# Five instead of four of the eight pairs of k tiles by seven products in the feed-forward units

## The chip, the cores and the metric

The kernel runs on one core of a Trainium2 chip. The metric is the device time of one execution in microseconds (us), lower is better. Before the change it is 2174.18 us, the median of three runs (2173.97 to 2175.04). The core has TensorE for matmuls (PE in the profile, its weight loads PEld), VectorE (DVE), ScalarE (ACT), GpSimd (POOL) and SyncE (SP), which issues the transfers from device memory. Each engine has its own queue, worked off in order.

## What is computed

Two layers of an encoder on 256 tokens of 2048 channels, all in float32. Each layer is a mixer (attention and a gated recurrence in the first, pooling and grouped attention in the second) and then a feed-forward, each with a residual sum and a normalisation. The change lies in the feed-forwards:

```python
def swiglu(x, w_gate, w_up, w_down):
    return (jax.nn.silu(x @ w_gate) * (x @ w_up)) @ w_down
...
x = layer_norm(DN_ALPHA * x + y, ln_mix_g[layer], ln_mix_b[layer])
f = swiglu(x, ffn_w_gate[layer], ffn_w_up[layer], ffn_w_down[layer])
x = layer_norm(DN_ALPHA * x + f, ln_ffn_g[layer], ln_ffn_b[layer])
```

`w_gate` and `w_up` are 2048 x 5632, `w_down` is 5632 x 2048.

## The kernel before

**Products.** A float32 operand is split into a high part, rounded to the type that TensorE takes (F32R), and a low part, the rest. `mm3` (line 289) makes one product of a 128 x 128 block of x, as the stationary operand, and a 128 x 512 block of weights from three matmuls: low by high, high by high, high by low. Weights come as "halves": two blocks of 128 x 512, 512 KB. `load_half` (line 147) transfers one into one of four buffers `raw`, ScalarE copies the high part into `whi` (line 122), VectorE subtracts it for the low part `wlo` (line 123). During the units the ring of `whi` and `wlo` has four buffers.

**The feed-forward's chunks.** The 5632 hidden columns are 11 chunks of 512. Chunks 0 and 1 are done by `whole`, plainly. Chunks 2 to 10 are "units" (`unit`, line 455), in rounds of two, `((2, 3), (0, 1)), ((4, 5), (2, 3))` and so on: while the units of a round make gate and up of two chunks, the down projection of the two chunks before runs in between, as steps of a generator (`down_steps`, line 508; a step is one half, 12 matmuls). There are nine units per layer, 18 in all.

**A unit.** It has four accumulator banks: c11 and c21 for the gate of the first and the second 128 tokens, c12 and c22 for the up. The 16 k tiles of x are eight pairs. A pair that is done plainly takes 2 token blocks x 2 k tiles x 2 (gate, up) = 8 products, 24 matmuls, from two halves. A pair done "by seven products" (pairs 4 to 7, `SEVEN`) uses sums: of x, the forms e, f, g, h, and of the weights. It comes in two parts.

- *The first phase.* `load_seven` (line 433) transfers the pair's four blocks in one piece of 1 MB (`rs`, two buffers), and VectorE makes sums of them in `z` (one buffer; lines 444 to 446). The gate block and three sums are split into `sh` and `sl` (two buffers each), the fourth sum, the "edge", into `zh` and `zl` (four buffers), which must live until the second phase. Four products (`BEGIN`, line 453) go into the four banks. After each pair come as many down steps as `GAPS` says: 2, 1, 1, 2. After the last pair ScalarE and VectorE combine the banks (lines 474 to 479): c12 is rewritten by line 476, c21 by line 478, c22 by line 479.
- *The second phase.* For each of the four seven-product pairs, one half of it is loaded again and split, and three products follow, into c11, c12 and (with the edge) c21. In between stand the four plain pairs. Then line 503 and 504 make silu(gate) times up; its transposition into `y` is left to a list, `flips`, which the next unit works off after its first two down steps.

So a unit has 48 + 132 matmuls of its own, and 96 of eight down steps: two before the flips, six in the gaps.

**Forms.** `forms_of` (line 409) makes e to h from x for the four pairs during the second chunk of `whole`, two steps at a time each time that a half has been used. Its tiles `xs` and `fs` take the room of `rs` and `z`.

**Buffers of y.** The transposed results y of the chunks, and before that the four groups of the mixer's result, share four buffers of 4 KB a partition for the high and the low part each (`new_yT`).

**Order of work.** The program is written in the order above, with raised priority for loads and splits (`tc.high_priority`). A planner then orders every engine's queue at build time: it plays the program through with costs of its own and takes at each point the first instruction that is ready, so matmuls of down steps and of later products fill in where weights are not ready. On the chip each queue keeps that order.

Of the kernel before, what the change touches and what calls it, by code (L numbers as in the profile page):

```python
# [12 lines left out]
F32R = mybir.dt.float32r  # L13
# [5 lines left out]
P = 128  # L19
T = 256  # L20
# [3 lines left out]
NCH = 512  # L24
# [45 lines left out]

ROUNDS = (((2, 3), (0, 1)), ((4, 5), (2, 3)), ((6, 7), (4, 5)), ((8, 9), (6, 7)), ((10,), (8,)))
LAST = (9, 10)
SEVEN = (4, 5, 6, 7)
PLAIN = (0, 1, 2, 3)
GAPS = (2, 1, 1, 2)


@with_exitstack
def trunk(ctx: ExitStack, tc: tile.TileContext, a, out):
# [5 lines left out]
    ap_ = ctx.enter_context(tc.tile_pool(name="acts", bufs=1))  # L85
# [11 lines left out]
    def bank(tag, bufs):  # L97
        return banks["pool"].tile([P, NCH], F32, tag=tag, name=tag, bufs=bufs)
# [22 lines left out]
    def split(hi, lo, src):  # L121
        nc.scalar.copy(hi, src)  # L122
        return nc.vector.tensor_tensor(lo, src, hi.bitcast(F32), op=sub).ins  # L123
# [55 lines left out]
    def half_done(n=1):  # L179
        for entry in list(later):  # L180
            entry[0] -= n
            if entry[0] <= 0:
                later.remove(entry)
                entry[1]()
# [70 lines left out]
        return xh, xl  # L255

    def new_yT():
        yh = ap_.tile([P, 4, T], F32R, tag="yTh", name="yTh", bufs=4)
        yl = ap_.tile([P, 4, T], F32R, tag="yTl", name="yTl", bufs=4)
        return yh, yl  # L260

    def x_lhs(xT):
        return lambda tok, k: (xT[0][tok][:, k, :], xT[1][tok][:, k, :])
# [18 lines left out]
    def split_tile(pool, shape, src, tag, bufs=1):  # L282
        hi = pool.tile(shape, F32R, tag=tag + "h", name=tag + "h", bufs=bufs)
        lo = pool.tile(shape, F32R, tag=tag + "l", name=tag + "l", bufs=bufs)
        if src is not None:
            split(hi, lo, src)
        return hi, lo
# [8 lines left out]
    def at(pair, *ix):  # L296
        return pair[0][ix], pair[1][ix]
# [108 lines left out]
        return xT  # L406


    def forms_of(sp, xT, out):

        n = len(SEVEN)
        xs = sp.tile([P, NT, 2 * n, P], F32, tag="rs", name="xs", bufs=2)
        fs = sp.tile([P, 4, n, P], F32, tag="z", name="fs", bufs=1)
        yield
        for t in range(NT):
            s = slice(2 * SEVEN[0], 2 * SEVEN[0] + 2 * n)
            nc.vector.tensor_tensor(xs[:, t], xT[0][t][:, s, :].bitcast(F32), xT[1][t][:, s, :].bitcast(F32), op=add)
            yield
        x11, x12, x21, x22 = (xs[:, t, e : 2 * n : 2, :] for t in range(2) for e in range(2))
        e, f, g, h = (fs[:, i] for i in range(4))  # L420
        nc.vector.tensor_tensor(e, x22, x21, op=sub)
        nc.vector.tensor_tensor(f, e, x11, op=add)
        yield
        nc.vector.tensor_tensor(g, x11, x21, op=sub)
        nc.vector.tensor_tensor(h, x12, f, op=sub)
        yield
        hi, lo = split_tile(sp, [P, 4, n, P], fs, "fm")
        for i, p in enumerate(SEVEN):
            x = lambda t, k: (xT[0][t][:, k, :], xT[1][t][:, k, :])
            e, f, g, h = (at((hi, lo), slice(None), j, i) for j in range(4))  # L430
            out[p] = {"11": x(0, 2 * p), "12": x(0, 2 * p + 1), "22": x(1, 2 * p + 1), "e": e, "f": f, "g": g, "h": h}

    def load_seven(sp, src):

        with tc.high_priority(offset=400):
            raw = sp.tile([P, 4, NCH], F32, tag="rs", name="rs", bufs=2)
            hi = sp.tile([P, 4, NCH], F32R, tag="sh", name="sh", bufs=2)
            lo = sp.tile([P, 4, NCH], F32R, tag="sl", name="sl", bufs=2)
            zh = sp.tile([P, NCH], F32R, tag="zh", name="zh", bufs=4)
            zl = sp.tile([P, NCH], F32R, tag="zl", name="zl", bufs=4)  # L440
            z = sp.tile([P, 4, NCH], F32, tag="z", name="z", bufs=1)
            last_load[0] = nc.sync.dma_start(raw, src).ins
            nc.scalar.copy(hi[:, 0], raw[:, 0])
            nc.vector.tensor_tensor(z[:, :2], raw[:, 0:3:2], raw[:, 3:4].to_broadcast([P, 2, NCH]), op=add)
            nc.vector.tensor_tensor(z[:, 2], z[:, 0], raw[:, 2], op=add)  # L445
            nc.vector.tensor_tensor(z[:, 3], z[:, 2], raw[:, 1], op=add)
            nc.vector.tensor_tensor(lo[:, 0], raw[:, 0], hi[:, 0].bitcast(F32), op=sub)
            split(hi[:, 1:], lo[:, 1:], z[:, :3])
            split(zh, zl, z[:, 3])
        return lambda i: (hi[:, i, :], lo[:, i, :]), (zh, zl)  # L450
# [4 lines left out]
    def unit(sp, w, lhs, forms, y, down, flips):  # L455


        def run(n):
            for _ in range(n):
                next(down, None)  # L460

        run(2)
        while flips:
            flips.pop(0)()
        b = {n: bank("un", 4) for n in ("c11", "c12", "c22", "c21")}
        edge = {}
        for i, (p, gap) in enumerate(zip(SEVEN, GAPS)):
            wt, edge[p] = load_seven(sp, w[p])
            for j, x, name in BEGIN:
                mm3(b[name], forms[p][x], wt(j), i == 0, i == len(SEVEN) - 1)  # L470
            if i == len(SEVEN) - 1:
                with tc.high_priority(offset=1000):
                    g0, g1 = (sp.tile([P, NCH], F32, tag=n, name=n, bufs=1) for n in ("g0", "g1"))
                    nc.scalar.copy(g0, b["c11"])
                    nc.vector.tensor_tensor(g1, b["c12"], g0, op=sub)
                    nc.vector.tensor_tensor(b["c12"], g1, b["c22"], op=sub)
                    nc.vector.tensor_tensor(g1, g1, b["c21"], op=sub)
                    nc.scalar.activation(b["c21"], g1, AF.Copy, scale=-1.0)
                    nc.vector.tensor_tensor(b["c22"], g1, b["c22"], op=sub)
            run(gap)  # L480

        left = {n: 4 * len(PLAIN) // 2 + (n != "c22") * len(SEVEN) for n in b}

        def product(name, x, wt):
            left[name] -= 1
            mm3(b[name], x, wt, False, left[name] == 0, skip_group_check=True)

        for p, s in zip(PLAIN, SEVEN):
            hi, lo = load_half(w[s][:, 1:3])
            for i, x, name in ((0, "12", "c11"), (1, "h", "c12")):  # L490
                product(name, forms[s][x], (hi[:, i, :], lo[:, i, :]))
            product("c21", forms[s]["22"], edge[s])
            half_done()
            for n, ks in ((0, (2 * p, 2 * p + 1)), (1, (2 * p + 1, 2 * p))):
                hi, lo = load_half(w[p][:, 2 * n : 2 * n + 2])
                for tok in range(NT):
                    for kk in range(2):
                        product(f"c{tok + 1}{n + 1}", lhs(tok, ks[kk]), (hi[:, kk, :], lo[:, kk, :]))
                half_done()
        with tc.high_priority(offset=1000):  # L500
            for tok in range(NT):
                g = sp.tile([P, NCH], F32, tag=f"g{tok}", name=f"g{tok}", bufs=1)
                nc.scalar.activation(g, b[f"c{tok + 1}1"], AF.Silu)
                nc.vector.tensor_tensor(g, g, b[f"c{tok + 1}2"], op=mult)
                s = slice(tok * P, (tok + 1) * P)
                flips.append(lambda g=g, s=s: transpose4(g, y[0][:, :, s], y[1][:, :, s], 1000))
# [31 lines left out]
    def ffn(layer, xT, res, mix_pool, close_mix, keep, last):  # L538
        lhs = x_lhs(xT)
        w = a[f"gu{layer}"]  # L540
# [33 lines left out]
        forms, making, sps, flips = {}, [], [], []  # L574

        def make():
            with tc.issue_after(low[-1]):
                for _ in range(2):
                    if next(making[0], "end") == "end":
                        return  # L580
            later.append([1, make])

        def change_rooms():
            close_mix()
            sps.append(later_pool(stack, f"sp{layer}"))
            making.append(forms_of(sps[0], xT, forms))
            later.append([1, make])

        groups = {c: None for c in range(2)}
# [20 lines left out]
        yl = y_lhs([groups[c] for c in LAST])  # L610
# [459 lines left out]


    xT = new_xT()
    yT = [new_yT() for _ in range(4)]
    with tc.tile_pool(name="wab", bufs=1) as wab:
        rings.append((wab, 2))
        with tc.tile_pool(name="ab", bufs=1) as mp:
# [7 lines left out]
    def later_pool(stack, name):  # L1084
        return stack.enter_context(tc.tile_pool(name=name, bufs=1, reuse_waits="tile"))
# [20 lines left out]

    consts = []
    xT = layer_end(0, a["ab_out"], AB_OUT_GROUPS, yT, False)
    yT = [new_yT() for _ in range(4)]
    with tc.tile_pool(name="cd", bufs=1, reuse_waits="tile") as mp:  # L1110
        cd_mixer(mp, consts, xT, yT)
    layer_end(1, a["cd_out"], CD_OUT_GROUPS, yT, True)
# [115 lines left out]
```

## Time and profile before

| | |
|---|---|
| median of three runs | 2174.18 us |
| the profiled execution: its own time | 2174.19 us |
| its span, first to last instruction | 2172.4 us |
| granted TensorE clock, mean | 0.997 |
| TensorE busy | 2152.8 us, 99% |
| VectorE busy | 1634.4 us, 75% |
| ScalarE busy | 1188.5 us, 55% |
| moved by DMA | 458.40 MB, 211 GB/s over the span |

The profile is one execution. Its time is 1.8 us over its span; work is counted against the time, positions are in us from the span's start. In a row of a group, "x72" is the number of instructions, then stand the busy time in all, the mean of one in ns, and the idle time of the engine before them with what ended it. In a row of the timeline stand the start, the duration, the engine, the line and what is written from what; a bracket gives the idle time before it and its releaser. A matmul's own duration (389 ns) overlaps with its neighbours', so its share of time is read from the distance of starts.

### The profile page before, as it was taken

What the parts mean: (1) busy time and instruction counts of PE and PEld (TensorE: products, weight loads), DVE (VectorE), ACT (ScalarE), POOL (GpSimd) and SP (SyncE); (2) the same over time, 40 slices, a digit from 0 to 9 for tenths busy, and PEclk for the clock granted to TensorE, in tenths of its full rate; (3) what the DMA queues carried; (4) which work ended last, traced back from release to release, by engine and by line L of the source; (5) the groups of instructions that cost most, each with busy time, mean ns of one, the idle gap of its engine ahead of it and who ended that gap; (6) DMA issues with size and microseconds to landing.
All of it is one profiled execution on the core that took longest, in us unless ns stands there. A gap on an engine that the chain in (4) does not pass through costs nothing.

```text
span 2172.4 us, 27036 instructions
## 1 busy us (share of the span) xinstructions
PE 2152.8 (99%) x9964; PEld 1790.4 (82%) x9964; DVE 1634.4 (75%) x2102; ACT 1188.5 (55%) x1586; POOL 57.4 (3%) x51
## 2 busy tenths in 40 slices
PE   9999999999999999999999999999999999999997
PEld 7888888888888888888888788888888888888886
DVE  6886688677797777887775876676878877777867
ACT  6445534555465565666554654454655666555652
POOL 0000001000000000000000300000000000000000
PEclk9999999999999999999999999999999999999999
DMA  8545545584677666766656663555767666666744
GB/s 295 162 164 181 163 142 181 188 290 141 213 243 237 229 235 232 244 236 214 236 194 234 202 203 122 200 190 187 253 233 241 242 227 213 240 230 234 242 161 169
DMA packets 119188, 458.40 MB, mean 211 GB/s; under 512 B 14480, under 2 KB 17552, under 8 KB 108560
## 3 DMA queue, kind: packets, MB, share of 16 engines
q1 hardware_dynamic: 119056, 456.68, 62.2%
q8 instruction: 78, 1.28, 0.2%
q14 instruction: 54, 0.44, 0.1%
HBM read 454.53 MB, written 2.10 MB: 210 GB/s over the span
## 4 chain that ended last, share of the span: by engine, by line
PE 97%; DVE 1%; DMA 0%; ACT 0%; issue 0%; SPq 0%; POOL 0%; DVEq 0%; ACTq 0%
PE acc L292 52%; PE un L292 34%; PE mx L292 7%; PE mx L786 1%; PE tr L119 1%; PE un L119 1%; PE mx L832 0%; PE mx L1045 0%; DVE wlo L123 0%; DMA raw<-in_ab_in 0%; PE mx L119 0%; DMA raw<-in_down 0%; ACT whi L122 0%; DVE xTl L370 0%; PE mx L1028 0%
## 5 line engine op out<-in xcount | busy, mean ns | idle before, releaser
L123 DVE TENSOR_TENSOR wlo<-raw,whi 128x1024 fp32r<-128x1024 f32 (+1 forms) x689 | 838.5, 1223 | 366.7 <-ACT whi L122 332.4
L122 ACT CAST whi<-raw 128x1024 fp32r<-128x1024 f32 (+1 forms) x689 | 721.8, 1052 | 703.0 <-PE acc L292 380.7
L292 PE MATMUL acc<-whi,yTl 128*128 128x512 f32 x896 | 349.2, 390 | 0.2
L292 PE MATMUL acc<-whi,yTh 128*128 128x512 f32 x896 | 348.9, 389 | 0.0
L292 PE MATMUL acc<-wlo,yTh 128*128 128x512 f32 x896 | 348.0, 390 | 0.1
L292 PE MATMUL acc<-whi,xTl 128*128 128x512 f32 x800 | 318.6, 398 | 5.2 <-ACT whi L122 5.0
L292 PE MATMUL acc<-whi,xTh 128*128 128x512 f32 x800 | 315.4, 394 | 0.0
L292 PE MATMUL acc<-wlo,xTh 128*128 128x512 f32 x800 | 313.0, 394 | 0.1
L292 PE MATMUL un<-whi,xTl 128*128 128x512 f32 x648 | 252.1, 389 | 0.0
L292 PE MATMUL un<-whi,xTh 128*128 128x512 f32 x648 | 252.1, 389 | 0.0
L292 PE MATMUL un<-wlo,xTh 128*128 128x512 f32 x648 | 245.9, 389 | 0.0
L292 PEld LDWEIGHTS acc<-wlo,yTh 128*128 128x128 f32 x896 | 168.2, 188 | 35.6 <-DVE wlo L123 0.8
L292 PEld LDWEIGHTS acc<-whi,yTl 128*128 128x128 f32 x896 | 168.2, 188 | 35.4 <-DVE res L308 0.5
L292 PEld LDWEIGHTS acc<-whi,yTh 128*128 128x128 f32 x896 | 168.2, 188 | 34.6
L292 PEld LDWEIGHTS acc<-whi,xTl 128*128 128x128 f32 x800 | 151.2, 189 | 35.5 <-ACT whi L122 5.8
L292 PEld LDWEIGHTS acc<-wlo,xTh 128*128 128x128 f32 x800 | 151.2, 189 | 31.2 <-DVE wlo L123 0.7
L292 PEld LDWEIGHTS acc<-whi,xTh 128*128 128x128 f32 x800 | 151.4, 189 | 28.8
L292 PEld LDWEIGHTS un<-wlo,xTh 128*128 128x128 f32 x648 | 121.6, 188 | 25.3
L292 PEld LDWEIGHTS un<-whi,xTl 128*128 128x128 f32 x648 | 121.6, 188 | 25.3
L292 PEld LDWEIGHTS un<-whi,xTh 128*128 128x128 f32 x648 | 121.6, 188 | 25.3
L123 DVE TENSOR_TENSOR sl<-z,sh 128x1536 fp32r<-128x1536 f32 x72 | 126.4, 1756 | 14.5 <-ACT sh L122 13.9
L122 ACT CAST sh<-z 128x1536 fp32r<-128x1536 f32 x72 | 106.5, 1479 | 7.7 <-DVE z L445 7.7
(241 smaller groups left out, 2648.8 us busy)
## 6 DMA issues: line engine op xcount, KB each, us to landing
raw<-in_gu SPq DMA_DIRECT2D x280, 512.0 KB, 4.5
raw<-in_down SPq DMA_DIRECT2D x176, 512.0 KB, 4.3
rs<-in_gu SPq DMA_DIRECT2D x72, 1024.0 KB, 7.1
raw<-in_ab_in SPq DMA_DIRECT2D x127, 512.0 KB, 4.2
raw<-in_cd_in SPq DMA_DIRECT2D x40, 512.0 KB, 4.3
raw<-in_ab_out SPq DMA_DIRECT2D x32, 512.0 KB, 4.5
raw<-in_cd_out SPq DMA_DIRECT2D x32, 512.0 KB, 4.4
bias<-in_na_bias SPq DMA_DIRECT2D x32, 64.0 KB, 3.9
```

Of the source, the lines that this page charges most:

```text
L119: return nc.tensor.transpose(o, src, eye)
L122: nc.scalar.copy(hi, src)
L123: return nc.vector.tensor_tensor(lo, src, hi.bitcast(F32), op=sub).ins
L292: ins = nc.tensor.matmul(o, lhs[a], rhs[b], start=start and n == 0, stop=stop and n == 2, **more)
L786: nc.tensor.matmul(m[:, 2 * h + s, :], kk[:, h, s * P : (s + 1) * P], qq[:, h, r * P : (r + 1) * P], start=True, stop=True,)
```

## The change

Pairs 3 to 7 instead of 4 to 7 are done by seven products, and pairs 0, 1 and 2 plainly. `GAPS` becomes 1, 1, 1, 1, 2, so a unit still has eight down steps. The second phase no longer alternates but follows `ORDER`, 3, 0, 4, 5, 1, 6, 7, 2.

Room is found in y: it has three buffers, and what was the fourth is a tile of its own, `y4h` and `y4l` (`fourth`). The mixers use it as the fourth group of their result. In a unit it holds the edges of the fourth and the fifth pair; `zh` and `zl` have three buffers for the first three. The forms are made by two generators one after the other, for pairs 3 to 5 into tiles `fm` and for pairs 6 and 7 into `fn`, and `make` goes on to the second when the first has ended.

```diff
-SEVEN = (4, 5, 6, 7)
-PLAIN = (0, 1, 2, 3)
-GAPS = (2, 1, 1, 2)
+SEVEN = (3, 4, 5, 6, 7)
+GAPS = (1, 1, 1, 1, 2)
+ORDER = (3, 0, 4, 5, 1, 6, 7, 2)
...
     def new_yT():
-        yh = ap_.tile([P, 4, T], F32R, tag="yTh", name="yTh", bufs=4)
-        yl = ap_.tile([P, 4, T], F32R, tag="yTl", name="yTl", bufs=4)
+        yh = ap_.tile([P, 4, T], F32R, tag="yTh", name="yTh", bufs=3)
+        yl = ap_.tile([P, 4, T], F32R, tag="yTl", name="yTl", bufs=3)
         return yh, yl
+
+    def fourth():
+
+        return tuple(ap_.tile([P, 4, T], F32R, tag=n, name=n, bufs=1) for n in ("y4h", "y4l"))
...
-    def forms_of(sp, xT, out):
+    def forms_of(sp, xT, out, seven, tag):
...
-    def load_seven(sp, src):
+    def load_seven(sp, src, room):
...
-            zh = sp.tile([P, NCH], F32R, tag="zh", name="zh", bufs=4)
-            zl = sp.tile([P, NCH], F32R, tag="zl", name="zl", bufs=4)
+            zh, zl = room or (sp.tile([P, NCH], F32R, tag=n, name=n, bufs=3) for n in ("zh", "zl"))
...
         for i, (p, gap) in enumerate(zip(SEVEN, GAPS)):
-            wt, edge[p] = load_seven(sp, w[p])
+            if i == 3:
+                room = [x.rearrange("p (e a) t -> p e (a t)", e=2) for x in fourth()]
+            wt, edge[p] = load_seven(sp, w[p], room and [x[:, i - 3] for x in room])
...
-        for p, s in zip(PLAIN, SEVEN):
-            hi, lo = load_half(w[s][:, 1:3])
-            for i, x, name in ((0, "12", "c11"), (1, "h", "c12")):
-                product(name, forms[s][x], (hi[:, i, :], lo[:, i, :]))
-            product("c21", forms[s]["22"], edge[s])
-            half_done()
+        for p in ORDER:
+            if p in SEVEN:
+                hi, lo = load_half(w[p][:, 1:3])
+                for i, x, name in ((0, "12", "c11"), (1, "h", "c12")):
+                    product(name, forms[p][x], (hi[:, i, :], lo[:, i, :]))
+                product("c21", forms[p]["22"], edge[p])
+                half_done()
+                continue
             for n, ks in ((0, (2 * p, 2 * p + 1)), (1, (2 * p + 1, 2 * p))):
...
                     if next(making[0], "end") == "end":
-                        return
+                        making.pop(0)
+                        if not making:
+                            return
...
-            making.append(forms_of(sps[0], xT, forms))
+            making.append(forms_of(sps[0], xT, forms, SEVEN[:3], "fm"))
+            making.append(forms_of(sps[0], xT, forms, SEVEN[3:], "fn"))
...
-    yT = [new_yT() for _ in range(4)]
+    yT = [new_yT() for _ in range(3)] + [fourth()]
```

More of the change, by code (lines that the diff above doesn't have):

```diff
@@ L406, in out_proj @@
         return xT
-    def forms_of(sp, xT, out):
-        n = len(SEVEN)
+    def forms_of(sp, xT, out, seven, tag):
+        n = len(seven)
         xs = sp.tile([P, NT, 2 * n, P], F32, tag="rs", name="xs", bufs=2)
@@ L415, in forms_of @@
         for t in range(NT):
-            s = slice(2 * SEVEN[0], 2 * SEVEN[0] + 2 * n)
+            s = slice(2 * seven[0], 2 * seven[0] + 2 * n)
             nc.vector.tensor_tensor(xs[:, t], xT[0][t][:, s, :].bitcast(F32), xT[1][t][:, s, :].bitcast(F32), op=add)
@@ L426, in forms_of @@
         yield
-        hi, lo = split_tile(sp, [P, 4, n, P], fs, "fm")
-        for i, p in enumerate(SEVEN):
+        hi, lo = split_tile(sp, [P, 4, n, P], fs, tag)
+        for i, p in enumerate(seven):
             x = lambda t, k: (xT[0][t][:, k, :], xT[1][t][:, k, :])
@@ L465, in unit @@
         b = {n: bank("un", 4) for n in ("c11", "c12", "c22", "c21")}
-        edge = {}
+        edge, room = {}, None
         for i, (p, gap) in enumerate(zip(SEVEN, GAPS)):
-            wt, edge[p] = load_seven(sp, w[p])
+            if i == 3:
+                room = [x.rearrange("p (e a) t -> p e (a t)", e=2) for x in fourth()]
+            wt, edge[p] = load_seven(sp, w[p], room and [x[:, i - 3] for x in room])
             for j, x, name in BEGIN:
@@ L480, in unit @@
             run(gap)
-        left = {n: 4 * len(PLAIN) // 2 + (n != "c22") * len(SEVEN) for n in b}
+        left = {n: 2 * (8 - len(SEVEN)) + (n != "c22") * len(SEVEN) for n in b}
         def product(name, x, wt):
@@ L1108, in trunk @@
     xT = layer_end(0, a["ab_out"], AB_OUT_GROUPS, yT, False)
-    yT = [new_yT() for _ in range(4)]
+    yT = [new_yT() for _ in range(3)] + [fourth()]
     with tc.tile_pool(name="cd", bufs=1, reuse_waits="tile") as mp:
```

## The prediction

> **What bounds the kernel now.** I read the page first, then who waits for whom on TensorE, then the chain of waits in order of time, then one unit in the timeline. The page's first lines and its chain:
>
> ```profile
> span 2172.4 us, 27036 instructions
> PE 2152.8 (99%) x9964; PEld 1790.4 (82%) x9964; DVE 1634.4 (75%) x2102; ACT 1188.5 (55%) x1586; POOL 57.4 (3%) x51
> PEclk9999999999999999999999999999999999999999
> PE 97%; DVE 1%; DMA 0%; ACT 0%; issue 0%; SPq 0%; POOL 0%; DVEq 0%; ACTq 0%
> ```
>
> TensorE is busy for 99% of the span at full granted clock, and 97% of the chain that ended last is TensorE. The table of who waited, TensorE's rows (total, times, longest):
>
> ```profile
> PE acc L292 <- ACT whi L122: 5.0, 2, 4.8
> PE un L292 <- DVE un L476: 0.3, 2, 0.2
> ```
>
> In the units (bank tag "un") TensorE waits 0.3 us in all, and for VectorE's rebuilding of bank c12 (line 476). That is where a late supply of weights would show first. The chain in order of time (start, length, what) shows two units' second phases:
>
> ```profile
> 826.21 29.92 PE un L292 x132
> 889.70 29.92 PE un L292 x132
> ```
>
> 132 matmuls take 29.92 us, so a matmul costs 0.2267 us, not the 0.389 us of its own row: neighbours overlap. The 132 are the second phase of a unit (4 pairs by three products = 36, 4 plain pairs by 24 = 96). The two starts are 63.49 us apart, one unit: 276 matmuls by 0.2267 = 62.6, and eight transposes.
>
> How full the engines are there (busy us of PE, PEld, DVE, ACT, POOL, then clock, DMA share, GB/s), for one unit, and for the stretch in which the forms are built ahead of the first unit:
>
> ```profile
> 828.40:891.90 63.50, 63.50 (x286) 52.64 (x285) 49.80 (x52) 37.81 (x47) 0.00 (x0) 1.00 0.68 232
> 570.00:608.00 38.00, 38.00 (x176) 31.53 (x175) 34.44 (x36) 20.41 (x23) 0.00 (x0) 1.00 0.77 260
> ```
>
> VectorE idles 13.7 us of a unit, ScalarE 25.7, DMA a third. VectorE is the next limit.
>
> **The change, part by part.** *Products.* A plain pair takes 8 products, a seven-product pair 7, each of three matmuls. One pair more per unit takes 3 matmuls away. The groups say how many units there are:
>
> ```profile
> L444 DVE TENSOR_TENSOR z<-rs 128x1024 f32<-128x1024 f32 x72 | 87.8, 1220 | 0.3
> L123 DVE TENSOR_TENSOR sl<-z,sh 128x1536 fp32r<-128x1536 f32 x72 | 126.4, 1756 | 14.5 <-ACT sh L122 13.9
> L122 ACT CAST sh<-z 128x1536 fp32r<-128x1536 f32 x72 | 106.5, 1479 | 7.7 <-DVE z L445 7.7
> L443 ACT CAST sh<-rs 128x512 fp32r<-128x512 f32 x72 | 44.7, 621 | 55.1 <-PE un L292 26.4 <-DMA rs<-in_gu 25.8 <-PE acc L292 2.8
> L122 ACT CAST zh<-z 128x512 fp32r<-128x512 f32 x72 | 44.5, 618 | 14.9 <-DVE z L446 14.0 <-PE un L292 0.8
> L122 ACT CAST whi<-raw 128x1024 fp32r<-128x1024 f32 (+1 forms) x689 | 721.8, 1052 | 703.0 <-PE acc L292 380.7
> rs<-in_gu SPq DMA_DIRECT2D x72, 1024.0 KB, 7.1
> ```
>
> x72 at four a unit is 18 units. 18 x 3 = 54 matmuls by 0.2267 us = **12.2 us** less on TensorE, on the path that sets the end.
>
> *Sums and splits on VectorE.* What an operation really takes from the queue is the distance from its start to the next start. VectorE's timeline in the unit that begins at 862.2:
>
> ```profile
> 870.67 0.69 DVE L447 TENSOR_TENSOR sl<-rs,sh 128x512 fp32r<-128x512 f32 x1 [0.61 <-ACT sh L443]
> 872.05 1.76 DVE L123 TENSOR_TENSOR sl<-z,sh 128x1536 fp32r<-128x1536 f32 x1 [0.68 <-ACT sh L122]
> ...
> 879.46 1.76 DVE L123 TENSOR_TENSOR sl<-z,sh 128x1536 fp32r<-128x1536 f32 x1 [0.20 <-ACT sh L122]
> 881.14 0.69 DVE L123 TENSOR_TENSOR zl<-z,zh 128x512 fp32r<-128x512 f32 x1
> 881.74 0.69 DVE L447 TENSOR_TENSOR sl<-rs,sh 128x512 fp32r<-128x512 f32 x1
> 882.34 1.22 DVE L444 TENSOR_TENSOR z<-rs 128x1024 f32<-128x1024 f32 x1
> 883.48 1.22 DVE L123 TENSOR_TENSOR wlo<-raw,whi 128x1024 fp32r<-128x1024 f32 x1
> ...
> 886.41 0.69 DVE L475 TENSOR_TENSOR g<-un,g 128x512 f32<-128x512 f32 x1 [0.38 <-PE un L292]
> ...
> 887.74 0.69 DVE L476 TENSOR_TENSOR un<-g,un 128x512 f32<-128x512 f32 x1
> 888.52 1.76 DVE L123 TENSOR_TENSOR sl<-z,sh 128x1536 fp32r<-128x1536 f32 x1
> ```
>
> 1.68 us for 1536 columns, 1.14 for 1024, 0.60 for 512. A seven-product pair has one of 1536, four of 512 (lines 445, 446, 447, zl), one of 1024 (line 444), and its reloaded half another 1.14: 6.36 us. A plain pair is two halves, 2.28. So VectorE gets **4.1 us more per unit**: 49.8 + 4.1 = 53.9 of 62.8 us, 86%. ScalarE gets 0.62 + 1.48 + 0.62 + 1.05 - 2 x 1.05 = 1.7 us more, against 25.7 idle. A unit's DMAs stay 24 in number and grow by 0.5 MB (1024 KB and a 512 KB half, for two halves), so 243 GB/s for 232, below the 260 of the second stretch: nothing, and if DMA were short it would show as late sums, costed next.
>
> *The first phase, with a gap of one step each.* The cover for the extra VectorE work must hold where VectorE has least room. The sums go one pair at a time, because z has one buffer and sh two. Starting from the ends of the three sl operations above, 873.81, 881.22 and 890.28, the slots are 7.4 and 9.1 us long. The third in before belongs to the next unit's first pair, whose use is 30 us off. After the change it belongs to this unit's fifth pair. It is longer because ScalarE stood before it with a copy whose transfer had not landed:
>
> ```profile
> 886.48 0.62 ACT L443 CAST sh<-rs 128x512 fp32r<-128x512 f32 x1 [1.59 <-DMA rs<-in_gu]
> 887.01 1.48 ACT L122 CAST sh<-z 128x1536 fp32r<-128x1536 f32 x1
> ```
>
> TensorE's side of that unit:
>
> ```profile
> 862.21 0.47 PE L292 MATMUL un<-sh,xTl 128*128 128x512 f32 x1
> 885.91 0.84 PE L292 MATMUL un<-sl,fmh 128*128 128x512 f32 x3
> 889.54 0.39 PE L292 MATMUL un<-whi,xTl 128*128 128x512 f32 x1
> 891.58 0.39 PE L292 MATMUL un<-whi,fml 128*128 128x512 f32 x1
> ```
>
> From 862.21 to 889.54 run 48 matmuls of the pairs and 72 of six down steps. After, 60 and 72, so the second phase starts at 892.3 and the first product on c12 (nine matmuls on c11 stand ahead of it now) at 894.3. The fifth pair's last three matmuls take 0.84 us after sl, lines 475 and 476 two more of 0.69: c12 stands 2.2 us after sl's end. With the slots as seen that is 888.6 + 2.2 = 890.8 (second slot again 7.4) to 890.28 + 2.2 = 892.5 (9.1). **It beats the need by 1.8 to 3.5 us**, so I cost this at nothing. Bounds: nothing below; above, one more half's wlo (1.14) in each of the two slots behind a 9.1 one, 10.2 us each: sl at 873.81 + 20.4 = 894.2, c12 at 896.4, 2.1 us late in every unit, 38 us in all. I take the near end since both slots were measured under the same queue. If this cover goes, what comes late next is c21 and c22 (lines 478, 479), and all plain products behind them.
>
> *Order of the second phase.* It shrinks from 132 to 117 matmuls. Neighbouring sevens (4, 5 and 6, 7) take 9 matmuls = 2.0 us a half of VectorE's 1.14; four ring buffers cover two of them. Nothing, by the same bounds.
>
> *Forms.* Two generators (three pairs, two pairs) for one, six steps more, in the second stretch above, where VectorE has 3.6 us idle. The rows of now (min/median/max ns):
>
> ```profile
> L417 DVE TENSOR_TENSOR xs<-xTh,xTl x4: 1215/1217/1220, 569.9 to 1514.3; 128x1024 f32<-128x1024 f32 x4
> L123 DVE TENSOR_TENSOR fml<-fs,fmh x2: 2292/2292/2293, 581.1 to 1524.4; 128x2048 fp32r<-128x2048 f32 x2
> ```
>
> That is 1.05 ns a column and 0.14 us each. Once 2 of 1024, 4 of 512, 1 of 2048: 7.4 us; then 2 of 768, 4 of 384, 1 of 1536 and 2 of 512, 4 of 256, 1 of 1024: 10.1. So 2.7 us more per layer, between 0 and 5.4 us in all. Both rs buffers hold xs meanwhile, so the first sums start later. I take 0.5 us per layer, near the covered end.
>
> *Buffers.* y's third and fourth use: the y of a unit is written after two down steps of the next unit, and the old chunk's last reader is the last down step of its round, at least a whole second phase (117 matmuls, 26.5 us) earlier. The fourth tile's sums are last read 24 matmuls before a unit's end and rewritten in the fourth pair of the next, behind 24 down matmuls and more: 11 us at least. Both nothing; uncovered, a y would cost two steps, 5.4 us, in eight units.
>
> *Sum.* The profiled execution took 2174.19 us (span 2172.4 and 1.8 around it), beside a median of 2174.18. 2174.2 - 12.2 + 1.0 = **2163.0 us**.
>
> **Rivals.** *Small stalls eat part.* The planner orders the queues anew and TensorE waits 0.2 to 0.9 us a unit at c12. For: line 476 is the one place with a wait now. Against: 1.8 us to spare. 2163 + 18 x 0.2 to 0.9 = 2167 to 2179.
>
> *Slower: the fifth pair's sums come late.* The mechanism is the upper bound above, at z's one buffer in the first phase; it decides once sl ends later than 892.1 (then c12 is late) and costs more than the gain from 892.8. For: VectorE is at 86% and this stretch has no idle to speak of; gaps fell to one step. At 10.2 us a slot: 2163 + 38 = 2201.
>
> *VectorE's idle is dependency, not room.* If its 13.7 us a unit could not be filled, each unit would grow by 4.1 us: 2174.2 + 18 x 4.1 = 2248. Against: TensorE hardly waits for it and most of the idle lies where full buffers hold ScalarE back. [...]
>
> *The three y buffers or the fourth tile bind after all*: 8 x 5.4 = 43, so 2206.
>
> **How the numbers follow.** A measurement of this kernel tells 0.2%, 4.3 us, from no change: faster is below 2169.8, slower above 2178.5. Forecast 0.60 (its own range 2160 to 2168). Small stalls 0.23, of which 0.07 stay faster and 0.16 are the same. Late sums 0.11, VectorE idle 0.03, buffers 0.03. Faster 0.67, same 0.16, slower 0.17. The range goes from 2159.5 (the 12.2 us and 2.5 of the 19.6 us in which TensorE is idle now, 2172.4 - 2152.8) to 2179, which leaves out the slower cases.
>
> **What would show it.** 9910 matmuls; a second phase of 117 matmuls in 26.5 us; units 62.8 us apart; VectorE near 54 us a unit; DVE and ACT 81 and 30 us more in all. Waits of "PE un" for line 476, sl or sh of 3 to 16 us in all would show the small stalls, more the late sums; more time between whole chunks and first unit, the forms. The prediction is wrong if units are over 63.2 us apart.

## The result, and the profile after

The changed kernel takes **2197.74 us** (2197.45 to 2198.12), beside 2174.14 for the kernel before on the same chip: a ratio of 1.0109 with a 95% interval of 1.0096 to 1.0121. It is slower by 23.6 us, where 11 us less were forecast (2163.0). Lines of the unit have moved: g1 (475) is now line 480, the rewriting of bank c12 (476) is line 481, and the sums z and lo0 are lines 447 to 450.

The page's first lines and its chain, as shown of before:

```profile
span 2196.4 us, 27084 instructions
PE 2147.0 (98%) x9910; PEld 1780.4 (81%) x9910; DVE 1710.7 (78%) x2206; ACT 1215.9 (55%) x1624; POOL 56.6 (3%) x51
PE 95%; DVE 3%; DMA 1%; ACT 0%; issue 0%; SPq 0%; POOL 0%; DVEq 0%; ACTq 0%
```

The 54 matmuls are gone (9964 to 9910). VectorE has 76 us more and ScalarE 27 us more, about what was expected (81 and 30). But 3% of the chain is now VectorE. The table of who waited, TensorE's row in the units (total, times, longest; its other rows are as before, or within 1.1 us):

```profile
PE un L296 <- DVE un L481: 29.0, 18, 3.4
```

TensorE waits for the rewriting of c12 in each of the 18 units, 29.0 us in all, where it was 0.3 us in two. The chain in order of time shows what releases one unit's first c12 product, and the next unit's:

```profile
837.77 0.62 DVE un L481
...
838.44 22.29 PE un L296 x97
...
903.23 2.83 PE un L296 x11
```

The two first c12 products are 64.79 us apart. A unit was forecast at 62.8. The window of one unit says the same (busy us of PE, PEld, DVE, ACT, POOL, then clock, DMA share, GB/s):

```profile
838.44:903.23 64.79, 63.11 (x282) 51.99 (x282) 54.05 (x58) 39.55 (x48) 0.00 (x0) 1.00 0.67 235
```

VectorE is busy for 54 us of a unit, just as forecast, and the clock is full (1.00). Each unit loses about 2 us, the first of each layer more (66.5 and 68.0 us long). In all, the span is 2196.4 instead of 2172.4 - 12.2 = 2160.2: **36.2 us are lost**, and 29.0 of them stand in the one row of waits. (That row undercounts: a matmul's modelled end, 0.39 us after its start, lies 0.16 us beyond the 0.2267 us at which the next would have started, so each wait hides about that much, 3 us in 18.)

Why is c12 late? TensorE's timeline of the unit that begins at 868.62:

```profile
868.62 0.47 PE L296 MATMUL un<-sh,xTl 128*128 128x512 f32 x1
...
897.98 0.39 PE L296 MATMUL un<-whi,xTl 128*128 128x512 f32 x1
...
900.02 0.84 PE L296 MATMUL un<-sl,fnh 128*128 128x512 f32 x3
...
901.15 0.39 PE L296 MATMUL un<-wlo,xTh 128*128 128x512 f32 x1
903.23 0.50 PE L296 MATMUL un<-whi,fml 128*128 128x512 f32 x1 [1.68 <-DVE un L481]
```

And VectorE's:

```profile
878.46 1.76 DVE L123 TENSOR_TENSOR sl<-z,sh 128x1536 fp32r<-128x1536 f32 x1 [0.69 <-ACT sh L122]
...
886.17 1.76 DVE L123 TENSOR_TENSOR sl<-z,sh 128x1536 fp32r<-128x1536 f32 x1 [0.52 <-ACT sh L122]
...
895.22 1.75 DVE L123 TENSOR_TENSOR sl<-z,sh 128x1536 fp32r<-128x1536 f32 x1
...
900.68 0.68 DVE L480 TENSOR_TENSOR g<-un,g 128x512 f32<-128x512 f32 x1
901.28 0.68 DVE L450 TENSOR_TENSOR sl<-rs,sh 128x512 fp32r<-128x512 f32 x1
901.88 0.68 DVE L449 TENSOR_TENSOR z<-z,rs 128x512 f32<-128x512 f32 x1
902.48 0.69 DVE L481 TENSOR_TENSOR un<-g,un 128x512 f32<-128x512 f32 x1
```

The fifth pair's sl ends at 896.97. The slots, from one sl's end to the next, were 7.7 and 9.04 us, close to the 7.4 and 9.1 of the forecast. By the forecast c12 stands 2.2 us after that, at 899.2; it stands at 903.17, **6.2 us after**. Two things lie between. On TensorE, nine matmuls (three products) on c11 of the second phase (897.98 to 900.02) come ahead of the fifth pair's last three, which c12 needs. On VectorE, line 481 starts 1.80 us after line 480 instead of 0.60, because two operations of the next unit's first sums (lines 450 and 449) stand between. After the last matmul that needs no c12 (901.15) the next was due at 901.38; it starts at 903.23, 1.85 us late. Neither order is forced by data: the planner that writes the queues at build time chose them. In the unit shown sl ends 29 us after the unit's transposes begin; about every second unit is like it, and in those between sl ends at 27 to 28 us and c12 comes 7.3 to 7.6 us later. The last unit of each layer has no next unit whose sums could stand in front of line 481: there it starts 0.80 us after line 480, and the wait is 0.45 us instead of 1.46 to 1.69 (2.92 and 3.41 in the first units).

### The profile page after: what moved, and what is told of

Read it like the earlier page. It is cut to its first block, busy times and chain, and to the rows that moved or that the text cites. A ratio compares the mean times of both kernels' runs of the same rounds, so it can differ in the third digit from the quotient of the medians.

```text
span 2196.4 us, 27084 instructions
## 1 busy us (share of the span) xinstructions
PE 2147.0 (98%) x9910; PEld 1780.4 (81%) x9910; DVE 1710.7 (78%) x2206; ACT 1215.9 (55%) x1624; POOL 56.6 (3%) x51
## 2 busy tenths in 40 slices
DMA packets 119190, 467.86 MB, mean 213 GB/s; under 512 B 14480, under 2 KB 17552, under 8 KB 106256
## 4 chain that ended last, share of the span: by engine, by line
PE 95%; DVE 3%; DMA 1%; ACT 0%; issue 0%; SPq 0%; POOL 0%; DVEq 0%; ACTq 0%
PE acc L296 52%; PE un L296 32%; PE mx L296 6%; PE mx L796 1%; PE tr L119 1%; PE un L119 1%; DVE un L481 1%; DVE sl L450 0%; DVE z L449 0%; DMA raw<-in_cd_in 0%; DVE g L480 0%; DVE wlo L123 0%; PE mx L842 0%; ACT whi L122 0%; PE mx L1055 0%
## 5 line engine op out<-in xcount | busy, mean ns | idle before, releaser
L296 PE MATMUL acc<-whi,yTl 128*128 128x512 f32 x832 | 324.1, 390 | 0.2
L296 PE MATMUL acc<-whi,yTh 128*128 128x512 f32 x832 | 324.0, 389 | 0.0
L296 PE MATMUL acc<-wlo,yTh 128*128 128x512 f32 x832 | 323.0, 390 | 0.2
L296 PE MATMUL un<-whi,xTl 128*128 128x512 f32 x522 | 203.7, 390 | 0.0
L296 PE MATMUL un<-whi,xTh 128*128 128x512 f32 x522 | 203.5, 390 | 0.0
L296 PE MATMUL un<-wlo,xTh 128*128 128x512 f32 x522 | 195.4, 390 | 0.0
L296 PEld LDWEIGHTS acc<-whi,yTh 128*128 128x128 f32 x832 | 156.2, 188 | 32.2
L123 DVE TENSOR_TENSOR sl<-z,sh 128x1536 fp32r<-128x1536 f32 x90 | 157.9, 1754 | 21.1 <-ACT sh L122 21.0
L122 ACT CAST sh<-z 128x1536 fp32r<-128x1536 f32 x90 | 132.9, 1477 | 17.8 <-DVE z L448 17.7
L296 PEld LDWEIGHTS un<-whi,xTl 128*128 128x128 f32 x522 | 98.3, 188 | 20.7
L296 PEld LDWEIGHTS un<-wlo,xTh 128*128 128x128 f32 x522 | 98.2, 188 | 20.7
```

Source lines behind the costliest of these rows:

```text
L296: ins = nc.tensor.matmul(o, lhs[a], rhs[b], start=start and n == 0, stop=stop and n == 2, **more)
```

## The experiments

Three theories were set against each other. The **order theory**: the time lies in where the planner put these few operations. The **load theory**: VectorE is simply too full with 4.2 us more per unit. The **buffer theory**: y's three buffers or the fourth tile bind. In the edits, `tc.issue_after` tells the planner to queue an instruction behind another one; under that condition the planner orders all queues anew. Each kernel was timed against the kernel before on its own chip, whose median lay between 2174.1 and 2174.7 us.

### Putting the orders right, one at a time

*pe_order*: on TensorE, the second phase's products may only be queued behind the last product of the first phase (`mm3` now returns its last matmul; the diff is abridged).

```diff
-                mm3(b[name], forms[p][x], wt(j), ...)
+                last_begin = mm3(b[name], forms[p][x], wt(j), ...)
...
         def product(name, x, wt):
             left[name] -= 1
-            mm3(b[name], x, wt, False, left[name] == 0, skip_group_check=True)
+            with tc.issue_after(last_begin):
+                mm3(b[name], x, wt, False, left[name] == 0, skip_group_check=True)
```

> The changed kernel with one edit: every product of a unit's second phase is queued on TensorE behind the last matmul of the first phase. Order theory: the fifth pair's sl stands 28 us into the unit as foreseen, but the planner put its last three matmuls behind nine products on c11 (2.04 us), so c12 is rewritten 2 us late. With the edit the nine products come after them and cover the rewriting: the wait for line 481 (1.6 us in each of 18 units) falls below 0.4 us, the time from 2197.7 to 2163 to 2171. Load theory (VectorE is simply too full, 54 of 64.8 us a unit): the order only shifts where TensorE waits, the time stays at 2192 or above. Buffer theory (three y buffers, the fourth tile): no effect, 2197.

Measured: 2181.64 us (2179.27 to 2182.96), ratio 1.0032 [1.0019, 1.0045]. That is 16.1 us back of 36, about half of what was expected (27 to 35). The slots of the fifth pair's sums are those of the changed kernel (7.7 and 9.04 us in the unit that begins at 864), so it is not earlier sums that gain. VectorE's timeline shows what is left:

```profile
896.45 0.68 DVE L481 TENSOR_TENSOR g<-un,g 128x512 f32<-128x512 f32 x1
897.05 0.68 DVE L451 TENSOR_TENSOR sl<-rs,sh 128x512 fp32r<-128x512 f32 x1
897.65 0.68 DVE L449 TENSOR_TENSOR z<-z,rs 128x512 f32<-128x512 f32 x1
898.25 0.69 DVE L482 TENSOR_TENSOR un<-g,un 128x512 f32<-128x512 f32 x1
```

The bank is summed up earlier, but the two operations of the next unit still stand between g1 (now line 481) and c12 (482). In the table of waits, line 482 still costs 11.0 us in 16 units.

*dve_order*: on VectorE, the next unit's first two `load_seven` are queued behind the rewriting of c12; TensorE's order stays as the change left it.

```diff
+    mended = []
...
-            wt, edge[p] = load_seven(...)
+            with ExitStack() as behind:
+                if mended and i < 2:
+                    behind.enter_context(tc.issue_after(mended[0]))
+                wt, edge[p] = load_seven(...)
...
-                    nc.vector.tensor_tensor(b["c12"], g1, b["c22"], op=sub)
+                    mended[:] = [nc.vector.tensor_tensor(b["c12"], g1, b["c22"], op=sub).ins]
```

> The changed kernel with one edit: VectorE's operations for the first two pairs of the next unit are queued behind the rewriting of c12 (line 481 of the changed kernel). Order theory: now two of them (0.6 us each) stand between lines 480 and 481; without them c12 comes 1.2 us earlier, the wait per unit falls from 1.6 to about 0.4 us, the time to 2173 to 2179. Load theory: VectorE does the same work, 2192 or above. Buffer theory: 2197.

Measured: 2189.82 us (2189.22 to 2190.72), ratio 1.0072 [1.0057, 1.0087]: 7.9 us back, where 19 to 25 were expected. The wait split in two:

```profile
PE un L297 <- DVE un L485: 10.0, 18, 1.4
PE un L297 <- ACT un L487: 8.1, 16, 0.5
```

c12 (line 485) is still late by TensorE's order, and what is mended behind it, c21 on ScalarE (line 487), is now late in its turn, as the prediction had named it for "what comes late next".

*both_orders*: both edits.

> The changed kernel with both edits of the queues' order, on TensorE and on VectorE. Order theory: no wait for the rewriting of c12 is left, the whole 12.2 us of the 54 matmuls is gained, 2161 to 2166. Load theory: 2190 or above.

Measured: 2171.63 us (2170.4 to 2172.58), ratio 0.9989 [0.9979, 0.9998]. The two orders together give back 26.1 us, about the sum of each alone (16.1 + 7.9 = 24.0); the forecast of 2161 to 2166 is missed by 6 us. TensorE no longer waits for c12; what remains in the units is c21, 3.9 us in 8 units, and 2.5 us for sh in two. ScalarE's and VectorE's rows of one such unit, then TensorE's:

```profile
893.88 0.70 DVE L486 TENSOR_TENSOR un<-g,un 128x512 f32<-128x512 f32 x1
894.49 1.22 DVE L449 TENSOR_TENSOR z<-rs 128x1024 f32<-128x1024 f32 x1
895.62 1.29 DVE L452 TENSOR_TENSOR sl<-rs,sh 128x512 fp32r<-128x512 f32 x2
896.83 0.68 DVE L487 TENSOR_TENSOR g<-g,un 128x512 f32<-128x512 f32 x1
...
898.01 1.05 ACT L122 CAST whi<-raw 128x1024 fp32r<-128x1024 f32 x1 [0.98 <-PE un L297]
898.98 0.59 ACT L488 ACTIVATE un<-g 128x512 f32<-128x512 f32 x1
899.62 0.50 PE L297 MATMUL un<-zh,xTl 128*128 128x512 f32 x1 [0.51 <-ACT un L488]
```

The same pattern one bank further on: the next unit's sums (lines 449, 452) went in right behind c12 (486) and ahead of line 487, from which c21 is made. And ScalarE's line 488 stood behind a half's whi copy that had itself waited 0.98 us for a ring buffer, with TensorE as its releaser.

### The rest put right

*mended_first*: both orders, and the next unit's sums go behind the last rewriting, that of c22, instead of c12 (the diff is against both_orders).

```diff
-                    mended[:] = [nc.vector.tensor_tensor(b["c12"], g1, b["c22"], op=sub).ins]
+                    nc.vector.tensor_tensor(b["c12"], g1, b["c22"], op=sub)
...
-                    nc.vector.tensor_tensor(b["c22"], g1, b["c22"], op=sub)
+                    mended[:] = [nc.vector.tensor_tensor(b["c22"], g1, b["c22"], op=sub).ins]
```

> The kernel with both orders, but the sums of the next unit's first two pairs are queued on VectorE behind the last of the four operations that rewrite the banks (c22), not behind the second (c12). With both orders TensorE was left with a wait for c21 in every other unit (0.5 us and what follows it, 0.8 us in all): the third operation stood behind 1.22 and two of 0.69 us of the next unit's sums, and ScalarE's write of c21 then behind a copy. Order theory: that wait goes too, units come 62.8 us apart and the time is 2161 to 2166. Load theory: VectorE's work is unchanged, so the wait only moves, 2170 or above.

Measured: **2165.51 us** (2164.91 to 2167.57), ratio 0.9962 [0.995, 0.9975], within the 2161 to 2166 expected. It is faster than the kernel before by 8.8 us, and than the changed one by 32.2. Its rows of engines and waits, and the window of one unit:

```profile
PE 2140.0 (99%) x9910; PEld 1777.5 (82%) x9910; DVE 1704.4 (79%) x2206; ACT 1204.7 (56%) x1624; POOL 51.4 (2%) x51
PE un L297 <- ACT sh L122: 2.4, 2, 1.2
923.40:986.20 62.80, 62.80 (x282) 51.91 (x281) 54.06 (x59) 38.67 (x48) 0.00 (x0) 1.00 0.69 244
```

The matmuls are the same as in the changed kernel, and VectorE is as busy (54.06 us in the unit shown). TensorE does not idle there, and the unit takes the 62.80 us forecast. Its timeline around the rewriting (VectorE's rows, and two of TensorE's), to be read against that of the changed kernel:

```profile
890.72 0.84 PE L297 MATMUL un<-sl,fnh 128*128 128x512 f32 x3
...
891.56 0.68 DVE L485 TENSOR_TENSOR g<-un,g 128x512 f32<-128x512 f32 x1
892.35 0.70 DVE L486 TENSOR_TENSOR un<-g,un 128x512 f32<-128x512 f32 x1
893.15 0.69 DVE L487 TENSOR_TENSOR g<-g,un 128x512 f32<-128x512 f32 x1
...
894.12 0.39 PE L297 MATMUL un<-whi,fml 128*128 128x512 f32 x1
```

Now c12 (486) ends at 893.05, 1.07 us before its first product starts. That is one of the five units with most to spare; in ten of the 18 it is 0.1 to 0.45 us, and in three 0.06 or less, one of these with a wait of 0.3 us. So the cover is thin. The sums do not come earlier than in the changed kernel: the fifth pair's sl ends 28 to 30 us after the unit's transposes begin (27 to 29 there; 31.9 in the first units of both), and the wait for c12 is all but gone even so. DMA traffic is the same as in the changed kernel too (467.86 MB), so neither earlier sums nor fewer transfers explain the 32 us.

*before_ordered*: the kernel before with the same three edits, to see whether the orders are worth something by themselves.

> The kernel before, four pairs, with the two orders of the fastest kernel so far: second-phase products behind the last matmul of the first phase, the next unit's first two pairs' sums behind the rewriting of the banks. Order theory: there was hardly a wait to take away (0.3 us), 2171 to 2177. If it gains as the five pairs did with them (32 us), the orders are worth something by themselves and the fifth pair is not what the gain comes from.

Measured: 2173.44 us (2172.52 to 2176.72), ratio 0.9996 [0.9987, 1.0005]: nothing clear of noise, as the order theory expected. In the kernel before no order needed mending; the gain of mended_first is the change's own.

### Taking the sums or the buffers apart

*no_fifth_sums*: the changed kernel, but the fifth pair makes no sums; its products use the fourth pair's. All matmuls remain.

```diff
-            wt, edge[p] = load_seven(...)
+            if i < 4:
+                wt, edge[p] = load_seven(...)
+            else:
+                edge[p] = edge[SEVEN[3]]
```

> The changed kernel, but the fifth pair's weights are neither loaded nor summed: it uses the fourth pair's sums and edge in their place (so the hidden values of the units are not the reference's). TensorE's work, the order of the products, the y buffers and the forms are the changed kernel's; VectorE has 5.2 us less per unit. Order theory and load theory: the stall is gone, 2160 to 2166. Buffer theory, or the order of the second phase as cause: the time stays above 2190.

Measured: 2161.03 us (2160.25 to 2162.65), ratio 0.994 [0.9925, 0.9955], 13.1 us below before. No row of the waits names c12. The chain in order of time:

```profile
1639.23 26.52 PE un L296 x117
...
1702.00 26.52 PE un L296 x117
```

The second phase of 117 matmuls takes 26.5 us and units are 62.77 us apart: the price of a matmul (0.2267 us) and the 12.2 us hold. y's three buffers and the fourth tile are all in this kernel, so the **buffer theory is out**, and with it the new `ORDER` of the second phase, which this kernel has as well. That the sums are gone does not tell their lateness from VectorE's load or from the 1 MB of transfer that went with them; mended_first, which keeps all three, does.

*four_in_new_room*: the changed kernel's buffers, fourth tile and two form generators, with four seven-product pairs in the old gaps.

```diff
-SEVEN = (3, 4, 5, 6, 7)
-GAPS = (1, 1, 1, 1, 2)
-ORDER = (3, 0, 4, 5, 1, 6, 7, 2)
+SEVEN = (4, 5, 6, 7)
+GAPS = (2, 1, 1, 2)
+ORDER = (4, 0, 5, 1, 6, 2, 7, 3)
...
-            if i == 3:
+            if i == 2:
...
-            making.append(forms_of(sps[0], xT, forms, SEVEN[:3], "fm"))
-            making.append(forms_of(sps[0], xT, forms, SEVEN[3:], "fn"))
+            making.append(forms_of(sps[0], xT, forms, SEVEN[:2], "fm"))
+            making.append(forms_of(sps[0], xT, forms, SEVEN[2:], "fn"))
```

> The changed kernel with four pairs by seven products again (gaps and order of products as before), but with all else of the change: three buffers of y, the fourth tile for the edges of the third and fourth pair, two generators of forms. Order theory and load theory: as before the change, 2172 to 2177. Buffer theory: above 2180.

Measured: 2176.49 us (2174.5 to 2177.51), ratio 1.001 [1.0001, 1.0019]. The new rooms cost about 2 us (0.2 to 4.1 by the interval), not 36: the buffers are off the list from the other side too.

### Load without the change

*load_in_second_phase*: the kernel before, with seven VectorE operations of 512 columns more per unit (4.2 us), whose result nobody reads, written in the second phase. The diff shows the operation; it is called after each seven-product pair of the second phase and three times in the plain pairs.

```diff
+        def extra():
+            s = sp.tile([P, NCH], F32, tag="g0", name="dm", bufs=1)
+            x = (dummy[0][j][0][:, 0:4, :].bitcast(F32) for j in range(2))
+            with tc.issue_after(low[-1]):
+                nc.vector.tensor_tensor(s.rearrange("p (k t) -> p k t", k=4), *x, op=add)
```

> The kernel before with seven more VectorE operations of 512 columns per unit, 4.2 us as the fifth pair brings, in the second phase, with results that nothing reads. Load theory: VectorE at 54 us a unit is what makes TensorE wait, at least 10 us slower, 2185 or above. Order theory: the place decides; the second phase has room for them, 2173 to 2178.

Measured: 2176.93 us (2175.71 to 2179.22), ratio 1.0015 [1.0006, 1.0024]. That is 2.7 us more, 0.15 us a unit, within the 2173 to 2178 of the order theory and far from the load theory's 2185.

*load_in_first_phase*: the same seven, written between the first phase's sums.

> The kernel before with the same seven operations per unit, but in the first phase, among the sums of the second to fourth pair, whose results nothing reads. Order theory: the fourth pair's sums come up to 4.2 us later, more than the 2 to 3 us by which c12 is early now, so a wait for line 476 appears in the units: 2180 to 2210. Load theory: the same amount as in the second phase.

Measured: 2173.19 us (2172.2 to 2175.39), ratio 0.9996 [0.9987, 1.0005]. The engines' row, and three rows of VectorE's timeline in one unit:

```profile
PE 2152.7 (99%) x9964; PEld 1790.5 (82%) x9964; DVE 1713.0 (79%) x2228; ACT 1187.2 (55%) x1586; POOL 52.4 (2%) x51
865.20 2.86 DVE L473 TENSOR_TENSOR dm<-xTh,xTl 128x512 f32<-128x512 f32 x4
...
886.96 0.68 DVE L485 TENSOR_TENSOR g<-un,g 128x512 f32<-128x512 f32 x1
...
888.91 0.69 DVE L486 TENSOR_TENSOR un<-g,un 128x512 f32<-128x512 f32 x1
```

VectorE is as full as in the changed kernel (1713.0 against 1710.7 us) and the time has not moved: the **load theory is out**. But the run does not test what it was sent for. The planner moved all seven operations to the unit's start, four of them at 865 us and all before 870.3, where nothing was due; the sums were hardly pushed, and the order theory's own expectation for this run (2180 to 2210) fell. Load that the planner was free to place cost nothing here (2173.19 us, beside 2174.27 for before), and says nothing about load that stands in the wrong place.

The last two rows say something else. Two operations of the next unit's sums (lines 448 and 447) stand between g1 (here line 485) and c12 (486) in this kernel too, 1.95 us from start to start, and nothing waits. With four pairs, sl ends 20.7 us after the unit's transposes begin, and c12 is done 1.6 us ahead of its first product. In no_fifth_sums the distance is even 2.3 us in most units, and c12 is 3.6 to 4.0 us ahead. So this order by itself costs nothing: it costs in the changed kernel because the fifth pair's sums end at 27 to 29 us and leave no room for it.

*late_4us* and *late_7us*: so the load was tied to the place. In the kernel before, the fourth pair's sum is rewritten onto itself by seven (or twelve) operations before it is split, so that it must come late. The diff is that of late_4us.

```diff
-    def load_seven(sp, src):
+    def load_seven(sp, src, again=0):
...
+            for _ in range(again):
+                nc.vector.tensor_tensor(z[:, 2], z[:, 2], z[:, 2], op=ALU.max)
...
-            wt, edge[p] = load_seven(sp, w[p])
+            wt, edge[p] = load_seven(sp, w[p], 7 if i == 3 else 0)
```

> The kernel before, four pairs; in each unit the fourth pair's sums are held up on VectorE by seven operations of 512 columns (4.2 us) that write a sum onto itself, ahead of its split. Now sl of this pair ends 8.3 us ahead of the second phase (881.2 of 889.5). Order theory: 4.2 us later it still ends 4 us ahead, more than the 2.2 us to c12, so little or no wait: 2174 to 2184. Load theory, already against two runs: 2185 or above.

> The same with twelve operations (7.2 us). Order theory: sl now ends about 1 us ahead of the second phase, as the fifth pair's does in the changed kernel (1.7 us ahead), and the planner's order adds its 3 to 4 us: a wait for line 476 of 1.5 to 2.5 us in each unit, 2200 to 2220, without a fifth pair. If lateness isn't the cause: below 2185.

Measured: 2270.04 us (2269.15 to 2270.83), ratio 1.044 [1.0424, 1.0455], and 2343.09 us (2341.5 to 2345.84), ratio 1.0773 [1.0755, 1.0791]. Both expectations are missed by far. The table of waits and VectorE's timeline in late_4us:

```profile
PE un L292 <- DVE un L478: 43.5, 18, 2.7
895.59 1.76 DVE L123 TENSOR_TENSOR sl<-z,sh 128x1536 fp32r<-128x1536 f32 x1 [0.69 <-ACT sh L122]
...
913.96 1.76 DVE L123 TENSOR_TENSOR sl<-z,sh 128x1536 fp32r<-128x1536 f32 x1 [0.64 <-ACT sh L122]
```

The lateness that was put in was not 4.2 us but 11: the slot between the two sl operations grew from 7.4 to 18.4 us, because beside the seven operations the planner put other work between the links of the chain (five splits of halves instead of two, for one). The runs show that a late fourth sum does lead to a wait at c12 (line 478 here): late_4us loses 5.3 us a unit in all, of which the row has 2.4. In late_7us the larger wait is another, for sh (70.2 us, beside 30.1 for c12). In late_4us two operations of the next unit stand in front of c12 as well (1.8 us from line 477 to 478), so these runs give no clean price per us of lateness.

## Why the prediction was wrong

**The step that failed** is "c12 stands 2.2 us after sl's end ... It beats the need by 1.8 to 3.5 us, so I cost this at nothing". It took the queues to run the operations in the order of need: sl, three matmuls, line 475, line 476. The changed kernel's queues have nine c11 matmuls in front of the three matmuls and two operations of the next unit's sums in front of c12, so that c12 came 6.2 us after sl's end and 1.85 us after its need. Binding these orders took the time from 2197.7 to 2181.6 (TensorE's), 2189.8 (VectorE's), 2171.6 (both), and 2165.5 us (with c21 and c22 put first as well): 32 of the 36 us lost. It takes both, the late sums and the orders: late sums with the orders put right (mended_first), or VectorE's order with sums that are not late (load_in_first_phase), cost little or nothing.

The prediction's own rows spoke against the 2.2 us. In the unit of before that they show, sl ends at 881.22 and line 476 at 888.43, **7.2 us** later. The three matmuls start only at 885.91, and line 476 starts 1.33 us after line 475, not 0.60, because an operation of the next unit's sums stands between them:

```profile
887.13 0.69 DVE L447 TENSOR_TENSOR sl<-rs,sh 128x512 fp32r<-128x512 f32 x1
```

In before this was covered, since the first product on c12 starts at 891.58, over 3 us after; so it was not read as a risk. With 7.2 us for 2.2 the same sum puts c12 at 895.8 to 897.5, which is 1.5 to 3.2 us after its need, or 2190 to 2221 us in all (an estimate from these rows; since c12 was not urgent in before, part of the 7.2 us may have been slack). Even mended_first takes 4.3 us from sl's end to c12's in most units, and no unit of it less than 3.1.

**The place was named, the mechanism was not.** The rival "the fifth pair's sums come late" had the place (c12), the size per unit (2.1 us; measured 2.0) and even the time (2201; measured 2197.7), at a chance of 0.11. Its mechanism, slots of 10.2 us, is not what happened in the unit shown: the slots were 7.7 and 9.04. Over the units they were 7.1 to 9.04 us, but for the first unit of each layer, where one of the two was 10.3. It was the near end of the bounds that came true for the slots, and a step costed without bounds behind it, the order within the queues, that set the time. That its time came within 4 us of the measured one was luck. "Small stalls", 0.2 to 0.9 us a unit at the same place, had the right mechanism ("the planner orders the queues anew") and half the size or less.

**Right by their own steps**: 54 matmuls by 0.2267 = 12.2 us (no_fifth_sums, with VectorE about as busy as before at 1620.2 us, is 13.1 below before, and its second phase takes the 26.5 us); units of 62.8 us once nothing waits (mended_first); VectorE at 54 us of a unit, with nothing lost by that alone (load_in_first_phase), so the rival "VectorE's idle is dependency, not room", 2248 us, is refuted in its general form; next to nothing for buffers (2 us in four_in_new_room); DMA at 235 (after) and 244 GB/s (mended_first), for 243 expected. In mended_first's unit VectorE is busy for 86% (54.06 of 62.80 us), and TensorE has no gap there; 4.2 us more of VectorE's work a unit cost nothing in load_in_first_phase.

**The forms** were priced at 0.5 us a layer for a late first unit. In no_fifth_sums the two generators cost nothing that can be seen. In mended_first the first unit of each layer takes 64.7 us, 1.9 over, and the two waits for sh (1.2 us each) lie there. The two layers make 3.8 of the 4.5 us that separate mended_first from no_fifth_sums. ScalarE's timeline in the first of these units:

```profile
634.75 0.59 ACT L484 COPY g<-un 128x512 f32<-128x512 f32 x1 [0.22 <-PE un L297]
635.23 0.61 ACT L532 ACTIVATE acc<-res 128x512 f32<-128x512 f32 x1
635.76 1.46 ACT L122 CAST sh<-z 128x1536 fp32r<-128x1536 f32 x1
```

The fifth pair's sh stands behind the copy of c11 and an activation of the whole chunk before the unit. So the loss lies at that pair's sums in the first unit, and it is four times the size that was taken. The rows look like a third order of the same kind; that it is the cause was not tried.

**Open**: of the changed kernel's 36.2 us, mended_first gives back 32.2 (by the medians), which are the orders; the 4.0 left are close to the first units' 3.8, whose cause was not tried. What a sum that comes a known time late costs, without any order of queues, is open: the runs meant for it missed their dose.

## What to carry to other kernels

An operation's place in its engine's queue can be a cost of its own. Here it cost nothing while the result had slack (load_in_first_phase: two operations of later work ahead of c12, and no wait for it), and 29.0 us of waits in the changed kernel, where the slack was gone. When a plan written at build time is made anew around a changed size, slack that was read from the old trace (here 1.8 to 3.5 us) holds only for the old order; before a cover is costed at nothing, read in the old trace how long the chain really took from its first link to its last (here 7.2 us, not the 2.2 of its own operations), list what else may be queued between its links, and price one or two such operations. When the engines' busy times come out as forecast and the time does not, read the two queues around the one growing wait for operations that belong to later work, and tie those behind the link that is due: here that turned 1.1% slower into 0.4% faster without one instruction of arithmetic changed.

## What the hardware showed that was not expected

After some of these waits TensorE itself ran slower: its matmuls started 0.43 us apart instead of 0.23. In late_4us the first matmul after a wait of 2.70 us and those that follow:

```profile
919.44 0.79 PE L292 MATMUL un<-whi,fml 128*128 128x512 f32 x1 [2.70 <-DVE un L478]
920.03 0.63 PE L292 MATMUL un<-whi,fmh 128*128 128x512 f32 x1
920.46 0.63 PE L292 MATMUL un<-wlo,fmh 128*128 128x512 f32 x1
...
922.56 0.40 PE L292 MATMUL un<-whi,xTh 128*128 128x512 f32 x1
922.80 0.40 PE L292 MATMUL un<-wlo,xTh 128*128 128x512 f32 x1
912.00:925.00 13.00, 10.10 (x36) 7.30 (x35) 11.44 (x13) 7.30 (x10) 0.00 (x0) 0.87 0.46 158
```

For about 3 us matmuls start 0.43 us apart, and the last row, a window over them, shows the granted clock at 0.87 on average. In this unit that makes some 1.4 us beside the wait itself (seven matmuls by 0.2 us). In another unit of late_4us, also after a wait of 2.70 us, the first three matmuls (from 781.72) start 0.33 us apart or less, and the slow starts come behind them: nine matmuls in the 3.65 us from 782.51 to 786.16, some 1.6 us over the usual. In the changed kernel a wait of 1.68 us (before 903.23) leaves the spacing at 0.23 but for the first start, and one of 2.92 us (before 644.54) too; the granted clock is 1.00 from 901 to 905 and from 643 to 653. After its wait of 3.41 us (before 1598.93) the next seven starts lie some 0.43 us apart, the first of them 0.60, and the clock is 0.55 from 1598.9 to 1602.5. So the length of the wait alone does not decide: slow starts followed 2.70 us twice in late_4us, and none followed 2.92 us in the changed kernel. What decides was not shown. This is a second price of a stall: in these two units of late_4us a wait of 2.70 us cost some 1.4 and 1.6 us more. Over the whole profiled execution the granted clock was 0.983 in late_4us, against 0.997 before.
